# Feed-forward part of a hybrid decoder layer: arithmetic moved off GpSimd, sums of weight blocks kept in DRAM

## The chip, the cores and the metric

One core of a Trainium2 chip runs the kernel. The time is the device time of one execution in microseconds, and a kernel's time is the median over its runs. The engines are named as the profile does: PE (matrix multiplications), PEld (loads of its stationary operand, which overlap PE), DVE (vector engine), ACT (activation engine), POOL (GpSimd) and SP (which here issues most transfers). Each engine takes its instructions in the order in which they were written for it and waits on semaphores for the others.

## The reference, cut to what matters

One layer is computed in float32 for a prompt of 2048 tokens and 8 single sample tokens, model width 1024, inner width 4096. Attention and retention come first and are not touched. The part that the change concerns is this:

```python
mix = jnp.einsum('bte,ed->btd', heads, w_out)
x1 = layernorm(ALPHA * x + mix, ln1_g, ln1_b)
h = jnp.square(jax.nn.relu(jnp.einsum('btd,df->btf', x1, w_up)))
ffn = jnp.einsum('btf,fd->btd', h, w_down)
y = layernorm(ALPHA * x1 + ffn, ln2_g, ln2_b)
```

`layernorm` subtracts the mean over the 1024 features, divides by the root of the variance plus 1e-5, and applies a gain and an offset.

## The kernel before

**Precision.** A float32 product is made of three matmuls with operands that are split in a high and a low part: `wh*xh + wh*xl + wl*xh`. `split` (L344 and L349) makes the high part on ACT by a copy with rounding, and the low part on DVE as the difference. So each weight tile and each activation tile costs one ACT and one DVE instruction.

**Layout.** Features lie on the partitions, tokens along the free dimension. The 2056 tokens are taken in three passes (`NPASS`) of 688, 688 and 680 columns, each of two halves (344, 344, 340 columns, `WIDTH`), so that a PSUM bank holds one half.

**Up product.** For a pair of inner-width blocks, `up_set` uses a Strassen-like scheme: the two halves of the tokens and two blocks of the weight form a 2x2 product from seven products instead of eight. Its activation side are seven combinations `fx` of x1 blocks (named in `ORD`), made once per pass by `build` and `build_jobs`. Its weight side are seven blocks of 128x512 that `f_prep` makes for each pair: four of them are parts of `w_up`, and three more sums and differences (`t`, `a21 + a22`, `a21 + a22 - a11`) and a fourth (`a12` less the last one) are computed on POOL from the two raw tiles (L288, L289, L290, L302). The same pairs of blocks are needed in each of the three passes, and the sums are made anew in each. `product` does one of the seven products, 12 matmuls, written as `ups` at L1577 to L1579. A *cell* adds the earlier products (L1601, DVE), applies relu (L1603, ACT), and `act` squares: ACT writes the rounded high part of the square into `hid` (L1588), POOL squares in place into `rl` (L1589), and DVE writes the difference into the low part (L1590).

**Down product.** `down` multiplies `hid` with tiles of `w_down` (`dps`, L1636 to L1638) and adds to `ya` in SBUF (L1645). The order of blocks in a pass is from `f_order`: two pairs of up blocks, then for each of the eight groups one up pair, the group's down product (16 accumulations of 12 matmuls), one up pair.

**Weights.** `f_load` requests the raw tiles in the order of the list `fraws` on SP's queue (L228), three tiles ahead, into four buffers of 128x1024. `f_prep` is called by `f_ahead` four products ahead of use, and its results go to six half-size buffers (`fu`), so that ACT and DVE can split up to six products ahead of PE. A request for a tile waits at SP until the splits of the tile that lay in its buffer are done, and all that SP issues later waits with it.

**Norms and builds beside the products.** Jobs of layer norm (`ln_jobs`) and of `build` are streams. Norm 2 of pass s-1, norm 1 of pass s+1 and the build for pass s+1 run during pass s; norm 1 of pass 0 and its build run during the output projection. `tick`, called twice in a product, advances a modelled time and hands out the next job of a stream when the modelled backlog of each engine that it uses (`tf`) is no more than 4 us (`AHEAD`); `busy` adds modelled costs of other work. A final scheduler then orders the instructions of each engine. A norm has: two chains of additions over the eight feature tiles (L1156 on POOL into `lb`, L1157 on DVE), their sum (L1159), its split, the mean by a matmul with ones (`lm`, L1171), the subtraction of the mean (L1182: tiles 1 and 5 on POOL, the rest on DVE), squares on ACT (L1185), their sum (L1178, alternately POOL and DVE), the variance by a matmul (`lvv`, L1199), and the scaling (L1208 on POOL for tiles 2 and 5, L1210 on DVE for the rest). In a build, two of four differences are on POOL, two on DVE (L1540).

**At a pass's end** the group 7 of passes 0 and 1 loads the 14 `fx` operands of the next pass from DRAM. POOL issues these transfers (L1709), and POOL also issues the loads of `ya` (L1675). Each waits until PE has used the old operand.

## Time and profile before

| | |
|---|---|
| median of 3 runs | 2728.62 us (2723.07 to 2729.89) |
| the profiled execution | 2731.33 us |
| its span, first to last instruction | 2729.5 us |
| mean granted TensorE clock | 0.976 |
| PE busy | 2615.8 us, 96% |
| DVE, ACT, POOL busy | 1862.1, 1173.3, 986.6 us |
| first up product of pass 0, last down product of pass 2 | 1245.3 us, 2718.3 us |

The busy shares are means over the whole span. The time before about 1150 us belongs to attention and retention and is the same in both kernels; of the rest, some stages hold only up and down products, and others hold norms and builds besides. The windows by stage in the prediction are cut along these.

### The profile page before, as it was taken

The page shows a single profiled execution, that of the slowest core. Times are in us where ns is not written, and L with a number is a line of the kernel's source. Part 1 is how long each engine was busy: PE and PEld are TensorE (multiplying, and loading weights), DVE is VectorE, ACT ScalarE, POOL GpSimd, SP SyncE. Part 2 cuts the span into 40 slices and gives each one's busy share as a digit, 9 for nine tenths or more (in the row PEclk, how much of TensorE's full clock was granted, in tenths as well). Part 3 has the DMA queues.
Part 4 walks back from the last instruction along what each step waited for, and adds up shares of the span by engine and source line. Part 5 has one row for each costly group of instructions (what it writes and reads, how often), then busy time and mean ns, then how long its engine had stood idle before and what let it go on. Part 6 is the DMA issues. An engine that isn't in the chain of part 4 may idle for free. (4 is left out here: it accounts for less than half of the span.)

```text
span 2729.5 us, 44870 instructions
## 1 busy us (share of the span) xinstructions
PE 2615.8 (96%) x16852; PEld 2409.8 (88%) x16852; DVE 1862.1 (68%) x3411; ACT 1173.3 (43%) x2420; POOL 986.6 (36%) x849
## 2 busy tenths in 40 slices
PE   8999999999999999987989999999999999999998
PEld 7998788767787887876989999999999999999997
DVE  4667876555777667488886555679886558865557
ACT  3455344343353555354553333345543324443325
POOL 2123533312332213145543333456533335433333
PEclk8999999999999999988999999999999999999999
DMA  7445765655664445675363221833562294322211
GB/s 243 125 128 171 215 191 153 212 185 166 182 199 151 136 136 180 188 248 194 104 225 122 84 72 62 321 108 104 168 224 79 70 266 146 129 75 81 78 62 57
DMA packets 211596, 412.23 MB, mean 151 GB/s; under 512 B 31745, under 2 KB 114434, under 8 KB 210835
## 3 DMA queue, kind: packets, MB, share of 16 engines
q1 hardware_dynamic: 193252, 363.94, 41.4%
q0 software_dynamic: 14880, 40.62, 4.7%
q10 hardware_dynamic: 3248, 4.82, 0.5%
q8 instruction: 133, 2.18, 0.3%
q14 instruction: 83, 0.68, 0.1%
HBM read 323.95 MB, written 85.35 MB: 150 GB/s over the span
## 5 line engine op out<-in xcount | busy, mean ns | idle before, releaser
L1637 PE MATMUL dps<-hid,fh 128*128 128x344 f32 (+2 forms) x1544 | 494.8, 321 | 6.9 <-DVE hid L1590 6.9
L1636 PE MATMUL dps<-hid,fh 128*128 128x344 f32 (+2 forms) x1544 | 491.2, 321 | 6.9 <-ACT fh L344 5.4
L1638 PE MATMUL dps<-hid,fl 128*128 128x344 f32 (+2 forms) x1544 | 485.3, 322 | 9.9 <-DVE fl L349 8.7
L1577 PE MATMUL ups<-fx,fu 128*128 128x344 f32 (+1 forms) x1344 | 436.9, 326 | 23.4 <-ACT fu L344 8.3
L1578 PE MATMUL ups<-fx,fu 128*128 128x344 f32 (+1 forms) x1344 | 436.1, 325 | 2.9 <-DVE fx L349 2.9
L1579 PE MATMUL ups<-fx,fu 128*128 128x344 f32 (+1 forms) x1344 | 428.3, 324 | 2.5 <-DVE fu L349 2.5
L336 PE MATMUL gps<-xh,wh 128*128 128x512 f32 (+2 forms) x1120 | 402.5, 362 | 8.0 <-ACT xh L344 6.9
L338 PE MATMUL gps<-xh,wl 128*128 128x512 f32 (+2 forms) x1120 | 399.6, 358 | 4.2 <-DVE wl L349 4.2
L337 PE MATMUL gps<-xl,wh 128*128 128x512 f32 (+2 forms) x1120 | 400.4, 358 | 1.1 <-DVE xl L349 0.8
L344 ACT ACTIVATE fu<-fr 128x512 fp32r<-128x512 f32 x288 | 176.3, 627 | 309.4 <-PE dps L1637 127.8
L1638 PEld LDWEIGHTS dps<-hid,fl 128*128 128x128 f32 x1544 | 292.7, 191 | 11.3 <-DVE fl L349 9.8
L1637 PEld LDWEIGHTS dps<-hid,fh 128*128 128x128 f32 x1544 | 294.6, 191 | 7.8 <-DVE hid L1590 7.8
L1636 PEld LDWEIGHTS dps<-hid,fh 128*128 128x128 f32 x1544 | 293.3, 190 | 8.7 <-ACT fh L344 6.5
L1645 DVE TENSOR_TENSOR ya<-dps,ya 128x344 f32<-128x344 f32 (+2 forms) x344 | 168.5, 501 | 174.3 <-PE dps L1638 173.0
L1577 PEld LDWEIGHTS ups<-fx,fu 128*128 128x128 f32 x1344 | 257.9, 192 | 28.8 <-ACT fu L344 9.5
L1589 POOL TENSOR_TENSOR rl<-rl 128x344 f32<-128x344 f32 (+1 forms) x192 | 184.9, 965 | 231.9 <-ACT hid L1588 231.8
L349 DVE TENSOR_TENSOR fu<-fr,fu 128x512 fp32r<-128x512 f32 x288 | 230.0, 811 | 52.1 <-ACT fu L344 50.6
L1578 PEld LDWEIGHTS ups<-fx,fu 128*128 128x128 f32 x1344 | 257.7, 192 | 4.3 <-DVE fx L349 4.2
L1579 PEld LDWEIGHTS ups<-fx,fu 128*128 128x128 f32 x1344 | 256.5, 192 | 3.8 <-DVE fu L349 3.8
L336 PEld LDWEIGHTS gps<-xh,wh 128*128 128x128 f32 x1120 | 215.1, 193 | 46.9 <-issue 8.7
L337 PEld LDWEIGHTS gps<-xl,wh 128*128 128x128 f32 x1120 | 215.5, 193 | 35.9 <-issue 7.5
L338 PEld LDWEIGHTS gps<-xh,wl 128*128 128x128 f32 x1120 | 215.8, 193 | 35.2 <-DVE wl L349 4.6
(263 smaller groups left out, 5146.5 us busy)
## 6 DMA issues: line engine op xcount, KB each, us to landing
wr<-in_w_in SPq DMA_DIRECT2D x111, 512.0 KB
fr<-in_w_up SPq DMA_DIRECT2D x96, 512.0 KB
fr<-in_w_down SPq DMA_DIRECT2D x96, 512.0 KB
xr<-in_x SPq DMA_DIRECT2D x64, 256.0 KB
wr<-in_w_out SPq DMA_DIRECT2D x32, 512.0 KB
t<-modd SPq DMA_DIRECT2D x16, 512.0 KB
ab<-ad SPq DMA_DIRECT2D x32, 256.0 KB
xr<-hd SPq DMA_DIRECT2D x32, 256.0 KB
```

Of the source, the lines that this page charges most:

```text
L336: mm(ps, wh, xh[:, c0:c0 + n], start=(k == 0), stop=False)
L337: mm(ps, wh, xl[:, c0:c0 + n], start=False, stop=False)
L338: mm(ps, wl, xh[:, c0:c0 + n], start=False, stop=(k == last))
L344: nc.scalar.activation(h, raw, AF.Copy)
L349: (nc.vector if eng_l == "v" else nc.gpsimd).tensor_tensor(out=l, in0=raw, in1=f32(h), op=OP.subtract)
L1577: mm(ps, wh, xh[:, k, :n], start=start and k == 0, stop=False, skip_group_check=not start)
L1578: mm(ps, wh, xl[:, k, :n], start=False, stop=False, skip_group_check=not start)
L1579: mm(ps, wl, xh[:, k, :n], start=False, stop=k == 3, skip_group_check=not start)
L1589: nc.gpsimd.tensor_tensor(out=r, in0=r, in1=r, op=OP.mult)
L1636: mm(ps, wh, xh, start=(k == 0), stop=False)
L1637: mm(ps, wh, xl, start=False, stop=False)
L1638: mm(ps, wl, xh, start=False, stop=(k == 3))
```

## The change

- `act`: ACT squares `rl` in place, then ACT copies it with rounding to the high part; POOL's instruction is gone.
- `ln_jobs` and `build_jobs`: all additions, subtractions and scalings are on DVE. POOL keeps only two scalings of the very last piece of the last norm, and some sums of squares in the last group's `down`.
- `f_prep`: in pass 0 the four sums of a pair of blocks are made on DVE, and each is stored by SP to a DRAM tensor `wsd` (16 of them, 4 blocks of 128x512 each). In passes 1 and 2 nothing is summed: the raw list has four tiles for a pair (the first `w_up` tile, two tiles of stored sums, the second half of the second `w_up` tile), and further requests are placed at pieces 3 and 4 of the seven.
- The modelled costs in `busy` and in the job lists follow the engines.

```diff
 def f_open(self):
+        self.wsd = [self.dram(f"wsd{p}", [P, 4, 512]) for p in range(16)]
...
-                    self.fraws += [self.i["w_up"][4 * g + f], self.i["w_up"][4 * g + f + 1]]
-                    self.funits += [("u", b, j) for j in range(7)]
+                    t, w = 4 * g + f, self.wsd[2 * g + f // 2]
+                    if s == 0:
+                        self.fraws += [up[t], up[t + 1]]
+                    else:
+                        self.fraws += [up[t], w[:, 0:2].rearrange("p a n -> p (a n)"),
+                                       w[:, 2:4].rearrange("p a n -> p (a n)"), up[t + 1][:, 512:1024]]
+                    self.funits += [("s" if s == 0 else "u", b, j, w) for j in range(7)]
...
 def f_prep(self, q):
-            pl(out=z["t"], in0=z["a11"], in1=z["a21"], op=OP.subtract)
-            pl(out=z["a21"], in0=z["a21"], in1=z["a22"], op=OP.add)
-            pl(out=z["a11"], in0=z["a21"], in1=z["a11"], op=OP.subtract)
-            src = z["a11"]
-            self.busy(P=3.9)
...
-            pl(out=z["a12"], in0=z["a12"], in1=z["a11"], op=OP.subtract)
...
+        if kind == "u":
+            t, c = ((0, 0), (1, 0), (0, 1), (1, 1), (2, 0), (3, 0), (2, 1))[j]
+            if j in (3, 4):
+                self.f_load(b + j + 1)
+            src = self.fraw[b + t][:, 512 * c:512 * c + 512]
...
+                v(out=z["t"], in0=z["a11"], in1=z["a21"], op=OP.subtract)
+                v(out=z["a21"], in0=z["a21"], in1=z["a22"], op=OP.add)
+                v(out=z["a11"], in0=z["a21"], in1=z["a11"], op=OP.subtract)
+                self.busy(D=2.1)
+            elif j == 6:
+                v(out=z["a12"], in0=z["a12"], in1=z["a11"], op=OP.subtract)
+                self.busy(D=0.7)
+            for k, o in {1: (("a11", 0),), 3: (("t", 1),), 4: (("a21", 2),), 6: (("a12", 3),)}.get(j, ()):
+                nc.sync.dma_start(ws[:, o, :], z[k])
...
 def ln_jobs(...):
-        app_p = APP_L if last else APP_P
+        app_p = APP_L if last else ()
...
-                    p(out=c["b"], in0=c["b"] if k else z[4], in1=z[5 + k], op=OP.add)
+                    v(out=c["b"], in0=c["b"] if k else z[4], in1=z[5 + k], op=OP.add)
...
-                    (v if k % 2 else p)(out=c[k - 1], in0=c[k - 1], in1=c[k - 3], op=OP.add)
+                    v(out=c[k - 1], in0=c[k - 1], in1=c[k - 3], op=OP.add)
...
-                    (p if k in CEN_P else v)(out=z[k], in0=z[k], in1=c["m"], op=OP.subtract)
+                    v(out=z[k], in0=z[k], in1=c["m"], op=OP.subtract)
...
 def build_jobs(...):
-        return [diff("P", t3, d, b), part("B11", a, 1), diff("P", b, b, a), part("B22", d, 1), part("T3", t3, 0),
+        return [diff("D", t3, d, b), part("B11", a, 1), diff("D", b, b, a), part("B22", d, 1), part("T3", t3, 0),
...
 def act(self, hid, c, n, r):
-        nc.scalar.activation(h, r, AF.Square)
-        nc.gpsimd.tensor_tensor(out=r, in0=r, in1=r, op=OP.mult)
+        nc.scalar.activation(r, r, AF.Square)
+        nc.scalar.copy(h, r)
         nc.vector.tensor_tensor(out=l, in0=r, in1=f32(h), op=OP.subtract)
-        self.busy(A=0.49, P=0.76, D=0.51)
+        self.busy(A=0.98, D=0.51)
```

Seven lines come in ahead of `split`, `ln_jobs` and `act`, so a line L349 of the old kernel is L356 in the new one, L1156 is L1163, L1590 is L1597, and L1709 is L1716.

POOL at the end of pass 1, before: the loads of `fx` (from DRAM tensors `xd2T` and `xd2B`) and the squares of the last cells (L1589) in one queue.

```order
L1709 DMA fx_23006<-xd2T_12468 128x4x340
L1709 DMA fx_23009<-xd2T_12471 128x4x340
L1589 TENSOR_TENSOR rl_22915<-rl_22915 128x344
L1709 DMA fx_23008<-xd2T_12470 128x4x340
L1589 TENSOR_TENSOR rl_22950<-rl_22950 128x344
L1709 DMA fx_23011<-xd2T_12473 128x4x340
L1709 DMA fx_23010<-xd2T_12472 128x4x340
L1709 DMA fx_23013<-xd2B_12475 128x4x340
L1709 DMA fx_23012<-xd2B_12474 128x4x340
L1589 TENSOR_TENSOR rl_22976<-rl_22976 128x344
L1589 TENSOR_TENSOR rl_22994<-rl_22994 128x344
```

The same place of POOL's queue in the changed kernel.

```order
L1716 DMA fx_23070<-xd2T_12468 128x4x340
L1716 DMA fx_23073<-xd2T_12471 128x4x340
L1716 DMA fx_23072<-xd2T_12470 128x4x340
L1716 DMA fx_23075<-xd2T_12473 128x4x340
L1716 DMA fx_23074<-xd2T_12472 128x4x340
L1716 DMA fx_23077<-xd2B_12475 128x4x340
L1716 DMA fx_23076<-xd2B_12474 128x4x340
```

The squares have left the queue, and the loads stand one behind the other.

POOL in the second norm of pass 2 (norm 2 of pass 1, second half), before: the chain of three additions into `lb_23923` (L1156), with block sums (L288 to L290, L302) around it.

```order
L290 TENSOR_TENSOR fr_23826<-fr_23895,fr_23826 128x512
L1156 TENSOR_TENSOR lb_23923<-zc_23864 128x344
L1156 TENSOR_TENSOR lb_23923<-lb_23923,zc_23864 128x344
L288 TENSOR_TENSOR ft_24274<-fr_23970,fr_24072 128x512
L302 TENSOR_TENSOR fr_23826<-fr_23826 128x512
L1156 TENSOR_TENSOR lb_23923<-lb_23923,zc_23864 128x344
L289 TENSOR_TENSOR fr_24072<-fr_24072 128x512
```

DVE at the same place in the changed kernel, where that chain is `lb_24060` (L1163), the other one is `lsq_24059` (L1164), and L1166 adds the two. L1650 is the down product's addition to `ya`.

```order
L1164 TENSOR_TENSOR lsq_24059<-zc_23987 128x344
L1650 SCALAR_TENSOR_TENSOR ya_23358<-ya_23358,dps_24038 128x340
L1164 TENSOR_TENSOR lsq_24059<-lsq_24059,zc_23987 128x344 x2
L1650 SCALAR_TENSOR_TENSOR ya_23358<-ya_23358,dps_24052 128x340
L1163 TENSOR_TENSOR lb_24060<-zc_23987 128x344
L1163 TENSOR_TENSOR lb_24060<-lb_24060,zc_23987 128x344 x2
L1650 SCALAR_TENSOR_TENSOR ya_23358<-ya_23358,dps_24072 128x340
L356 TENSOR_TENSOR fu_24192<-fr_23946,fu_24192 128x512
L1166 TENSOR_TENSOR lsq_24059<-lsq_24059,lb_24060 128x344
```

The second chain has come from POOL to DVE, where it follows the first one, with two other operations before their sum.

DVE at the opening of pass 0, before (first build, first weight blocks).

```order
L349 TENSOR_TENSOR fu_13549<-fr_13541,fu_13549 128x512
L349 TENSOR_TENSOR fx_12485<-zc_13232,fx_12484 128x344
L1540 TENSOR_TENSOR zc_13232<-zc_13232 128x344
L349 TENSOR_TENSOR fx_12479<-zc_13232,fx_12478 128x344
L349 TENSOR_TENSOR fx_12483<-lb_13379,fx_12482 128x344
L1340 SCALAR_TENSOR_TENSOR z_13469<-xr_13362,gps_13407 128x512
L1540 TENSOR_TENSOR zc_13232<-zc_13232 128x344
L349 TENSOR_TENSOR fu_13559<-fr_13541,fu_13559 128x512
```

And in the changed kernel, from the same first low part of a weight block on.

```order
L356 TENSOR_TENSOR fu_13565<-fr_13557,fu_13565 128x512
L301 TENSOR_TENSOR ft_13568<-fr_13557,fr_13559 128x512
L302 TENSOR_TENSOR fr_13559<-fr_13559 128x512
L1547 TENSOR_TENSOR lb_13345<-zc_13304 128x344
L356 TENSOR_TENSOR fx_12489<-zc_13304,fx_12488 128x344
L303 TENSOR_TENSOR fr_13557<-fr_13559,fr_13557 128x512
L356 TENSOR_TENSOR fx_12489<-zc_13304,fx_12488 128x344
L1547 TENSOR_TENSOR zc_13304<-zc_13304 128x344
L356 TENSOR_TENSOR fx_12483<-lb_13345,fx_12482 128x344
L356 TENSOR_TENSOR fu_13573<-fr_13557,fu_13573 128x512
```

Three block sums (L301 to L303) and the builds' differences of POOL (L1547) stand between the low parts that the first products need.

More of the change, by code (lines that the diff above doesn't have):

```diff
@@ L47 @@
 ORD = ("B11", "T2", "B21", "T3", "T1", "T4", "B22")
-CEN_P = (1, 5)
-APP_P = (2, 5)
 SP = 100
@@ L208, in f_open @@
                     self.fraws.append(self.i["w_down"][g, d])
-                    self.funits.append(("c" if s == NPASS - 1 and g == 7 else "d", b, d))
+                    self.funits.append(("c" if s == NPASS - 1 and g == 7 else "d", b, d, None))
         self.flr, self.fraw, self.fq, self.fp, self.frdy, self.fpar, self.fset = 0, {}, 0, 0, {}, 0, {}
@@ L227, in f_load @@
             t = pool.tile([P, 1024], F32, tag="wr", name=self.nm("fr"), bufs=2)
-            self.nc.sync.dma_start(t, self.fraws[q])
+            src = self.fraws[q]
+            t = t[:, :src.shape[-1]]
+            self.nc.sync.dma_start(t, src)
             self.fraw[q] = t
@@ L232, in f_slots @@
     def f_slots(self, q):
-        return 1 if self.funits[q][0] == "u" else 2
+        return 1 if self.funits[q][0] in "su" else 2
     def f_next(self):
@@ L256, in f_prep @@
         nc = self.nc
-        kind, b, j = self.funits[q]
-        pl = nc.gpsimd.tensor_tensor
-        if kind != "u":
+        kind, b, j, ws = self.funits[q]
+        v = nc.vector.tensor_tensor
+        if kind not in "su":
             self.f_load(b + 3)
@@ L1159, in f @@
                     v(out=c["a"], in0=c["a"], in1=c["b"], op=OP.add)
-            return f, [("P", G, 0)] * (k < 3) + [("D", D, 0)], 1
+            return f, [("D", D * (1 + (k < 3)), 0)], 1
         def parts(x):
@@ L1207, in f @@
                     if k in app_p:
-                        p(out=z[k], in0=z[k], in1=c["r"], op=OP.mult)
+                        nc.gpsimd.tensor_tensor(out=z[k], in0=z[k], in1=c["r"], op=OP.mult)
                     else:
```

36 lines of the change are left out of this document (14 added, 22 removed).

## The prediction

> **What bounds the kernel now.** I read the page's busy shares first, then the windows by stage (columns: length, then busy us and count of PE, PEld, DVE, ACT, POOL, the granted TensorE clock, DMA share, GB/s), then who PE waited for, then the DVE groups of the stages with gaps.
>
> ```profile
> PE 2615.8 (96%) x16852; PEld 2409.8 (88%) x16852; DVE 1862.1 (68%) x3411; ACT 1173.3 (43%) x2420; POOL 986.6 (36%) x849
> ...
> 1150.00:1245.00 95.00, 85.23 (x477) 74.26 (x476) 71.89 (x105) 42.51 (x76) 36.52 (x31) 0.93 0.78 263
> 1245.00:1310.00 65.00, 47.44 (x240) 42.29 (x238) 60.81 (x77) 31.68 (x66) 39.80 (x34) 0.86 0.41 143
> 1310.00:1460.00 150.00, 138.12 (x817) 135.28 (x818) 121.74 (x190) 72.58 (x143) 70.43 (x59) 0.95 0.53 180
> 1460.00:1710.00 250.00, 250.00 (x1587) 250.00 (x1587) 143.27 (x227) 87.08 (x153) 82.27 (x69) 1.00 0.22 72
> 1710.00:2040.00 330.00, 310.93 (x1899) 307.05 (x1898) 263.59 (x397) 155.32 (x305) 167.63 (x148) 0.97 0.54 186
> 2040.00:2195.00 155.00, 155.00 (x986) 155.00 (x985) 90.35 (x143) 54.12 (x94) 50.95 (x42) 1.00 0.23 75
> 2195.00:2350.00 155.00, 143.57 (x878) 141.53 (x878) 115.08 (x166) 67.20 (x128) 84.75 (x77) 0.96 0.65 198
> 2350.00:2655.00 305.00, 305.00 (x1961) 305.00 (x1960) 185.91 (x297) 108.57 (x191) 104.84 (x87) 1.00 0.26 85
> 2655.00:2730.00 75.00, 60.55 (x426) 59.09 (x424) 55.88 (x116) 38.81 (x94) 26.62 (x26) 0.93 0.18 58
> ```
>
> TensorE sets the end, and its instructions are the same before and after, some norm matmuls at other places. Where the feed-forward part runs alone (1460-1710, 2040-2195, 2350-2655) PE is busy all the time at clock 1.00: there an edit on another engine is worth nothing, unless it spoils this. Something is to be had only where layer norms and builds run beside it. Idle (length less PE busy) and clock loss (1 less the clock, times the length) are: out projection 9.8 + 6.7, opening of pass 0 17.6 + 9.1, its norms 11.9 + 7.5, pass 1 19.1 + 9.9, pass 2 11.4 + 6.2, end 14.5 + 5.3. That is 84 + 45 us, the most that any edit here could return. In these stages DVE is busy 74% to 94% of the time, so a wait that ends on DVE, or on ACT for a DVE result, is a queue on DVE.
>
> Why that queue is long:
>
> ```profile
> L349 DVE TENSOR_TENSOR fu<-fr,fu 128x512 fp32r<-128x512 f32 x65 | 52.8, 823 | 12.4 <-ACT fu L344 12.2
> L1590 DVE TENSOR_TENSOR hid<-rl,hid 128x344 fp32r<-128x344 f32 x42 | 35.0, 838 | 6.0 <-POOL rl L1589 6.0
> L1645 DVE TENSOR_TENSOR ya<-dps,ya 128x344 f32<-128x344 f32 x64 | 31.4, 506 | 8.9 <-PE dps L1638 8.8
> L349 DVE TENSOR_TENSOR fl<-fr,fh 128x1024 fp32r<-128x1024 f32 x20 | 26.9, 1346 | 4.1 <-PE ups L1579 3.2 <-ACT fh L344 0.9
> L1210 DVE SCALAR_TENSOR_TENSOR zc<-zc,lnp,lb 128x344 f32<-128x344 f32 (+1 forms) x24 | 23.8, 1058 | 0.0
> L1182 DVE TENSOR_TENSOR zc<-zc,lm 128x344 f32<-128x344 f32 (+1 forms) x24 | 15.2, 696 | 0.0
> L1178 DVE TENSOR_TENSOR lsq<-lsq,lsq 128x344 f32<-128x344 f32 (+1 forms) x12 | 10.1, 843 | 0.5 <-ACT lsq L1185 0.4
> ...
> L349 DVE TENSOR_TENSOR fu<-fr,fu x288: 675/692/2648, 1240.2 to 2672.6; 128x512 fp32r<-128x512 f32 x144
> L349 DVE TENSOR_TENSOR fl<-fr,fh x92: 1209/1226/2353, 1309.0 to 2630.8; 128x1024 fp32r<-128x1024 f32 x92
> L1590 DVE TENSOR_TENSOR hid<-rl,hid x192: 496/512/2276, 1269.9 to 2687.0; 128x344 fp32r<-128x344 f32 x128, 128x340 fp32r<-128x340 f32 x64
> L1645 DVE TENSOR_TENSOR ya<-dps,ya x344: 319/509/519, 1379.9 to 2718.6; 128x344 f32<-128x344 f32 x112, 128x340 f32<-128x340 f32 x52, 128x170 f32<-128x170 f32 x8
> L1210 DVE SCALAR_TENSOR_TENSOR zc<-zc,lnp,lb x60: 559/568/1625, 1204.1 to 2351.9; 128x344 f32<-128x344 f32 x48, 128x340 f32<-128x340 f32 x12
> ```
>
> The first seven rows are DVE groups of pass 1's stage (the number before the second bar is the mean ns), the last five the min/median/max of a line. The same 344-wide operation takes 496 ns at best, 838 on the mean in this stage and 2276 at worst where both inputs lie in SBUF, but never over 519 where one comes from PSUM. The delay therefore is in SBUF beside POOL's arithmetic. Per stage of pass 1 the excess over the medians is 65 x 0.131 = 8.5, 42 x 0.326 = 13.7, 20 x 0.12 = 2.4, 24 x 0.49 = 11.8, and with 0.512 as the free 344-wide duration 24 x 0.184 = 4.4 and 12 x 0.33 = 4.0: 44.8 us in 330.
>
> **The change part by part.** *POOL to DVE.* DVE gets 64 sums of 128x512 (pass 0 only, 64 x 0.692 = 44 us) and 138 operations of layer norm and build (138 x 0.512 = 71 us): 10 for each of ten norms, 14 in the parts of the last two, 8 for each of three builds. Pass 1 holds four norms and a build, 48 x 0.512 = 24.6 against the 44.8 that go: DVE falls from 263.6 to about 243 of 330. Pass 2's stage: POOL is busy 84.75 against 167.6, so about 22.7 go and 10.2 come (two norms). Pass 0 from 1245 to 1460: POOL 110, so about 29.5 go, while 8 pairs of blocks bring 8 x 4 x 0.692 = 22.1, two norms 10.2 and the builds some 7: 39. DVE is then about 9 us busier, 192 of 215.
>
> *Squares to ACT.* POOL's `rl` product goes; ACT makes the square in place and a copy more.
>
> ```profile
> L1589 POOL TENSOR_TENSOR rl<-rl x192: 745/934/1742, 1265.3 to 2685.2; 128x344 f32<-128x344 f32 x128, 128x340 f32<-128x340 f32 x64
> ...
> L1603 ACT ACTIVATE rl<-rl 128x344 f32<-128x344 f32 x93 | 45.2, 488 | 68.8 <-DVE rl L1601 68.2
> ```
>
> 192 copies by 0.488 are 94 us on ACT, hidden: pass 1's stage goes from 155 to about 176 of 330, pass 0's norms from 73 to 82 of 150. Without that cover the splits `fu` and `fh` behind them on ACT would be late by 0.49 each time. A cell's chain gets shorter by 0.934 - 0.488 = 0.45 us. What this frees is POOL's queue:
>
> ```profile
> 2212.08 0.74 POOL L1709 DMA_DIRECT2D fx<-xd2T  x1 [2.43 <-DMA fx<-xd2T]
> 2215.09 1.48 POOL L1709 DMA_DIRECT2D fx<-xd2B  x2 [2.26 <-issue]
> 2216.59 1.48 POOL L1589 TENSOR_TENSOR rl<-rl 128x344 f32<-128x344 f32 x2
> 2217.39 3.78 DVE L1590 TENSOR_TENSOR hid<-rl,hid 128x344 fp32r<-128x344 f32 x2 [5.93 <-POOL rl L1589]
> ...
> PE dps L1637 <- DVE hid L1590: 6.9, 2, 4.7
> ...
> 2210.00:2220.00 10.00, 5.29 (x33) 5.00 (x33) 4.07 (x4) 0.93 (x2) 5.56 (x7) 0.85 1.41 380
> 2220.00:2230.00 10.00, 10.00 (x53) 10.00 (x54) 6.83 (x11) 1.69 (x2) 0.99 (x2) 0.81 1.40 363
> ```
>
> At the end of a pass the last squares stand behind loads of the next operands, and PE waits 4.7 us (2.2 a pass earlier). These 6.9 us go whatever DVE does, with the clock lost in the last two rows, 1.5 + 1.9: **-10.3**.
>
> *The norm's sum.* The mean's matmul stands in PE's order and waits for a chain that goes over POOL:
>
> ```profile
> 2315.28 0.93 POOL L1156 TENSOR_TENSOR lb<-zc 128x344 f32<-128x344 f32 x1 [8.22 <-DMA zc<-yd]
> 2316.29 1.26 POOL L1156 TENSOR_TENSOR lb<-lb,zc 128x344 f32<-128x344 f32 x1
> 2317.51 1.75 POOL L288 TENSOR_TENSOR ft<-fr,fr 128x512 f32<-128x512 f32 x1
> ...
> 2320.43 0.91 POOL L1156 TENSOR_TENSOR lb<-lb,zc 128x344 f32<-128x344 f32 x1
> 2321.38 1.56 DVE L1159 TENSOR_TENSOR lsq<-lsq,lb 128x344 f32<-128x344 f32 x1 [2.02 <-POOL lb L1156]
> ...
> PE lm L1171 <- ACT lsq L344: 11.1, 5, 4.3
> ...
> PE lm L1171 <- ACT lsq L344: 2.6, 2, 2.0
> ```
>
> Three additions take from 2315.3 to 2321.3, with block sums between them (of the last two rows one is the whole run's, one pass 1's stage; the 4.3 is pass 2's). On DVE they come behind the other chain's three, with two other operations before the sum: 6 x 0.512 + 2 x 0.5 = 4.1 us instead of 6.1. I take half of the 11.1 us, 5.5, and half as much in clock (the table's 45 to 84): **-8**, bounds 0 and -16.6.
>
> *DVE's backlog in passes 1 and 2.* Of 30.5 us idle, 6.9 (squares) and 2.6 + 4.3 (lm) are spoken for; 16.7 is left. With 20 us less on DVE I take half and its clock: **-12**, bounds 0 and -25. *Pass 0.* Idle 29.5, clock 16.6, and DVE 9 us busier but without operations of up to 2.3 us: bounds -25 and +25, taken **-5** since a late part on the path had one hop less. *The rest* (end, out projection): -1, bounds -9 and +6.
>
> PE's longest wait in the stage 1310-1460 was:
>
> ```profile
> PE ups L1577 <- DVE u L1619: 3.3, 1, 3.3
> ```
>
> The Trainium skill's page TensorE: Matmul & The Clock Gate (What's actually happening) lets the clock fall only after an idle window of some 3.4 us. The stage 1310-1460 lost 7.5 us of clock with this as its longest wait, so the trace does not bear that out as a strict bound; by it the backlog's term would be some 2 us smaller and the result 2699.
>
> *Sums kept in DRAM.* Pass 0 stores 64 x 256 KB; a pair of blocks in passes 1 and 2 loads 1792 KB instead of 1024, 32 times: 16.8 + 25.2 = 42 MB more. SP issues them all.
>
> ```profile
> SPq L228 <- DVE fu L349: 704.5, 89, 23.9
> ```
>
> SP's queue already waits 704 us for raw buffers; behind its new stores stand the next loads. A product is 12 matmuls of 250/1587 = 0.158 us, 1.9 us; seven products with 1792 KB need 139 GB/s, below the 380 of the row 2210-2220. Raw tiles are now asked for four pieces ahead (7.6 us) besides the six that splits run ahead of PE. Only beside the loads at a pass's opening can that be short: **+2**, bounds 0 and +8.
>
> Sum: -10.3 - 8 - 12 - 5 - 1 + 2 = -34. The profiled execution took 2731.33 us (span 2729.5); 2731.3 - 34 = **2697**. The median of the runs shown, 2728.62, is 2.7 lower.
>
> **The rivals.** (a) *DVE becomes the bound in pass 0: slower.* For: 94% busy in the opening already; its idle there is 4.2 us and the 12 sums of three pairs of blocks alone bring 8.3; in 1310-1460 idle is 28.3 and about 28 come. If the excess does not go, the opening is 7 us longer and the next stage has no slack; I price that at half of 28 and half again in clock, 7 + 14 + 10 = 31. With passes 1 and 2 returning the sure 10.3, 2731 + 31 - 10 = 2752. It decides from about 145 of 150 us busy there. Against: the 496-to-2276 spread. The Trainium skill's Perfetto Trace Analysis (Optimizing Scalar/DVE Operations) advises moving work off a saturated DVE, which speaks for this rival; it adds that between DVE and GpSimd that might not help, as they share a port, which the spread bears out. (b) *Order, not load, makes the stalls*: each is a place in PE's order, new ones come where old ones go, and only the sure part stays, less the stores: 2731 - 10 + 5 = 2726. (c) *The relief is worth more*: a stall ends once a queue is shorter than the run-ahead; then the whole of the bounds for norm and backlog comes and half of pass 0's: 2731 - 10 - 17 - 25 - 13 = 2666. (d) *Loads become late* at each opening of pass 1 and 2, +8 and as much again in two places: 2731 - 34 + 18 = 2715. That POOL's arithmetic stays is excluded: 8 instructions of it are left in this part.
>
> **How the numbers follow.** Forecast 0.50, (c) 0.18, (d) 0.05, (b) 0.13, (a) 0.14. Within 0.3% (8 us, what repeated runs can tell) of 2728.6 lies (b); faster is 0.50 + 0.18 + 0.05 = 0.73, slower 0.14. The range reaches from a little below (c) to (b): 2660 to 2728; the forecast's own is 2682 to 2712.
>
> **What would show it.** The 344-wide SBUF operations at means near 0.51; no wait of PE for `hid` at a pass's end; lm waits under 4 us in sum; DVE near 243 us in pass 1's norms; PE at 100% with clock 1.00 in the quiet stages. Wrong, if DVE is over 95% busy through 1310-1460 and PE idles there more than 12 us, or if `fu` waits for `fr` loads.

## The result, and the profile after

The changed kernel took 2651.86 us (median of 4 runs, 2645.22 to 2659.17), the kernel before 2726.7 us (4 runs): ratio 0.9727, 95% interval 0.9697 to 0.9756. The gain is 75 us where 34 were forecast. The direction was right; the time lies 8 us below the range and closest to rival (c).

The page of the changed kernel, busy time of each engine (span 2649.5 us):

```profile
PE 2583.2 (97%) x16852; PEld 2387.1 (90%) x16852; DVE 1776.2 (67%) x3613; ACT 1245.5 (47%) x2612; POOL 363.3 (14%) x327
```

DVE does 202 instructions more than before and is busy 86 us less. The same stages as in the prediction, in the windows of the changed kernel (length, then busy us and count of PE, PEld, DVE, ACT, POOL, granted clock, DMA share, GB/s):

```profile
1150.00:1234.00 84.00, 79.73 (x463) 69.69 (x463) 64.04 (x117) 38.98 (x69) 9.41 (x5) 0.98 0.85 281
1234.00:1297.00 63.00, 44.74 (x231) 40.34 (x230) 48.95 (x99) 34.74 (x74) 1.89 (x2) 0.78 0.60 202
1297.00:1450.00 153.00, 153.00 (x973) 153.00 (x972) 127.48 (x249) 86.18 (x172) 0.00 (x0) 1.00 0.60 205
1450.00:1700.00 250.00, 249.74 (x1583) 249.17 (x1582) 156.71 (x270) 107.09 (x198) 7.45 (x14) 1.00 0.42 146
1700.00:2015.00 315.00, 310.30 (x1953) 309.89 (x1952) 233.75 (x456) 175.48 (x354) 1.80 (x2) 0.99 0.60 203
2015.00:2165.00 150.00, 150.00 (x953) 150.00 (x953) 79.38 (x135) 60.31 (x110) 10.36 (x14) 1.00 0.46 145
2165.00:2310.00 145.00, 145.00 (x931) 145.00 (x930) 107.92 (x205) 77.13 (x157) 1.79 (x2) 1.00 0.65 217
2310.00:2585.00 275.00, 275.00 (x1767) 275.00 (x1766) 155.56 (x273) 112.91 (x211) 0.00 (x0) 1.00 0.31 102
2585.00:2650.00 65.00, 55.11 (x406) 54.48 (x405) 45.04 (x112) 38.70 (x97) 5.12 (x8) 0.96 0.24 76
```

The third row is the one to learn from. In the norms of pass 0 DVE is busy 127.48 of 153 us, 83%; before it was 121.74 of 150, 81%. PE lost 11.9 us there before and loses nothing now, with as full a DVE. Loss of a stage is length less PE busy, plus one less the clock times the length, as in the prediction:

| stage | loss before | after |
|---|---|---|
| out projection | 16.5 | 6.0 |
| opening of pass 0 | 26.7 | 32.2 |
| norms of pass 0 | 19.4 | 0 |
| norms of pass 1 | 29.0 | 7.9 |
| norms of pass 2 | 17.6 | 0 |
| end | 19.8 | 12.5 |

Most of the gain is in one stretch, from the first to the last down product. This is its row before, and then after:

```profile
1306.00:2718.00 1412.00, 1362.89 (x8542) 1352.74 (x8541) 974.83 (x1520) 580.54 (x1095) 587.99 (x506) 0.98 0.38 126
```

```profile
1297.00:2639.00 1342.00, 1337.04 (x8550) 1335.94 (x8548) 901.36 (x1682) 654.06 (x1286) 25.50 (x38) 1.00 0.48 162
```

It is 70 us shorter: PE idles 44 us less (49.1 to 5.0), and its matmuls take 26 us less (1362.89 to 1337.04), since the clock falls less often. The span fell by 80.0 us. Of the other 10, 11 came ahead of the first up product (1245.3 to 1234.4 us), and the opening, from there to the first down product, got 2 longer (60.3 to 62.7 us).

DVE of the changed kernel, four groups of pass 1's norms (1700 to 2015 us; mean ns before the last bar), and min/median/max of one line over the run:

```profile
L356 DVE TENSOR_TENSOR fu<-fr,fu 128x512 fp32r<-128x512 f32 x79 | 52.7, 687 | 7.1 <-ACT fu L351 6.8
L356 DVE TENSOR_TENSOR fl<-fr,fh 128x1024 fp32r<-128x1024 f32 x21 | 25.6, 1221 | 5.6 <-ACT fh L351 5.5
L1597 DVE TENSOR_TENSOR hid<-rl,hid 128x344 fp32r<-128x344 f32 x44 | 22.4, 511 | 1.9 <-ACT hid L1596 1.7
L1217 DVE SCALAR_TENSOR_TENSOR zc<-zc,lnp,lb 128x344 f32<-128x344 f32 x16 | 8.0, 572 | 0.7 <-ACT lb L1209 0.7
...
L1597 DVE TENSOR_TENSOR hid<-rl,hid x192: 502/509/524, 1268.5 to 2608.0; 128x344 fp32r<-128x344 f32 x128, 128x340 fp32r<-128x340 f32 x64
```

823 ns became 687, 1346 became 1221, 838 became 511, and 2276 at worst became 524. DVE operations with both inputs in SBUF are no longer held up. What PE still waits for between 1230 and 2650 us in the changed kernel (sum, count, longest):

```profile
PE ups L1584 <- ACT fx L351: 14.1, 3, 10.5
PE ups L1584 <- ACT p L1616: 6.8, 2, 4.7
PE ups L1584 <- ACT fu L351: 1.3, 2, 1.0
PE lvv L1206 <- DVE lsq L1658: 1.1, 1, 1.1
```

The waits for `hid`, `fl`, `fh`, `u` and, in this stretch, `lm` are gone. Two are new: 10.5 us for `fx` in the opening and 4.7 us at 1970 us.

### The profile page after: what moved, and what is told of

The parts are those of the page before. It is cut to its first block, busy times and chain, and to the rows that moved or that the text cites. A ratio compares the mean times of both kernels' runs of the same rounds, so it can differ in the third digit from the quotient of the medians.

```text
span 2649.5 us, 44699 instructions
## 1 busy us (share of the span) xinstructions
PE 2583.2 (97%) x16852; PEld 2387.1 (90%) x16852; DVE 1776.2 (67%) x3613; ACT 1245.5 (47%) x2612; POOL 363.3 (14%) x327
## 2 busy tenths in 40 slices
DMA packets 230028, 454.18 MB, mean 171 GB/s; under 512 B 33793, under 2 KB 116482, under 8 KB 229267
## 4 chain that ended last, share of the span: by engine, by line
PE 78%; DMA 9%; DVE 7%; issue 2%; POOL 1%; ACT 1%; SPq 1%; DVEq 0%; POOLq 0%; ACTq 0%
PE dps L1644 8%; PE dps L1645 8%; PE dps L1643 8%; PE ups L1584 7%; PE ups L1585 7%; PE ups L1586 7%; PE gps L343 5%; PE gps L345 5%; PE gps L344 5%; PE o L685 2%; PE ptps L654 2%; PE vps L439 2%; PE vps L440 2%; PE vps L441 2%; DMA zc<-x1d 1%
## 5 line engine op out<-in xcount | busy, mean ns | idle before, releaser
L351 ACT ACTIVATE fu<-fr 128x512 fp32r<-128x512 f32 x320 | 193.4, 627 | 339.4 <-PE dps L1644 226.1
L1644 PEld LDWEIGHTS dps<-hid,fh 128*128 128x128 f32 x1544 | 290.3, 188 | 0.0
L1643 PEld LDWEIGHTS dps<-hid,fh 128*128 128x128 f32 x1544 | 289.7, 188 | 0.1
L1584 PEld LDWEIGHTS ups<-fx,fu 128*128 128x128 f32 x1344 | 254.6, 190 | 25.3 <-ACT fx L351 15.2
L1585 PEld LDWEIGHTS ups<-fx,fu 128*128 128x128 f32 x1344 | 254.8, 190 | 2.4 <-DVE fx L356 2.4
L1586 PEld LDWEIGHTS ups<-fx,fu 128*128 128x128 f32 x1344 | 253.8, 190 | 0.8 <-DVE fu L356 0.8
L356 DVE TENSOR_TENSOR fu<-fr,fu 128x512 fp32r<-128x512 f32 x320 | 214.5, 689 | 45.4 <-ACT fu L351 43.8
L356 DVE TENSOR_TENSOR wl<-wr,wh 128x1024 fp32r<-128x1024 f32 (+1 forms) x147 | 189.8, 1297 | 57.7 <-ACT wh L351 55.3
```

Of the source, the lines that this page charges most:

```text
L351: nc.scalar.activation(h, raw, AF.Copy)
L356: (nc.vector if eng_l == "v" else nc.gpsimd).tensor_tensor(out=l, in0=raw, in1=f32(h), op=OP.subtract)
L1584: mm(ps, wh, xh[:, k, :n], start=start and k == 0, stop=False, skip_group_check=not start)
L1585: mm(ps, wh, xl[:, k, :n], start=False, stop=False, skip_group_check=not start)
L1586: mm(ps, wl, xh[:, k, :n], start=False, stop=k == 3, skip_group_check=not start)
L1643: mm(ps, wh, xh, start=(k == 0), stop=False)
```

## The experiments

**The question.** The theory after the result: what cost PE its time was DVE's *hold-up* beside POOL's reading of SBUF, not DVE's load. One rival is DVE's load, the prediction's own measure; another that PE waited for POOL's results and for what stood behind them in POOL's queue. Hold-up below means: over all additions, subtractions and multiplications of DVE between the first and the last down product, the sum of duration less the free duration of the shape, where it is over 15 ns (688 ns at 512 wide, 1220 at 1024, 507 and 502 at 344 and 340, 562 and 560 in the scalar form). It is worked out from the single instructions of each trace. All gains below are against the runs of the kernel before in the same comparison, whose median was 2719.85 to 2726.7 us.

| kernel | ratio, 95% interval | gain, us | first to last down product, us | PE idle there | DVE busy | POOL busy | hold-up |
|---|---|---|---|---|---|---|---|
| before | 1 | 0 | 1412 | 49.1 | 975 | 588 | 155 |
| squares alone | 0.992 (0.9895 to 0.9945) | 24 | 1387 | 34.7 | 936 | 394 | 119 |
| norms alone | 0.9899 (0.9868 to 0.993) | 25 | 1382 | 31.0 | 971 | 479 | 109 |
| sums alone | 0.9816 (0.9789 to 0.9843) | 52 | 1362 | 19.5 | 938 | 320 | 86 |
| sums back on POOL | 0.978 (0.9757 to 0.9803) | 57 | 1351 | 13.0 | 927 | 280 | 66 |
| norms back on POOL | 0.9758 (0.9727 to 0.9789) | 69 | 1351 | 11.7 | 906 | 143 | 52 |
| squares back on POOL | 0.9753 (0.9733 to 0.9774) | 66 | 1349 | 10.2 | 928 | 202 | 32 |
| changed, idle POOL reads | 0.9734 (0.9716 to 0.9752) | 70 | 1342 | 4.9 | 936 | 206 | 39 |
| changed, idle POOL writes | 0.9732 (0.9708 to 0.9757) | 71 | 1342 | 4.8 | 901 | 167 | 1 |
| changed, three times the idle POOL work | 0.9908 (0.9884 to 0.9931) | 24 | 1383 | 34.4 | 1051 | 571 | 160 |
| changed | 0.9727 (0.9697 to 0.9756) | 75 | 1342 | 5.0 | 901 | 26 | 1 |
| changed, sums on DVE in every pass | 0.9711 (0.9687 to 0.9735) | 80 | 1335 | 0.5 | 974 | 26 | 1 |
| changed, `ya` later | 0.9699 (0.9682 to 0.9715) | 80 | 1339 | 4.3 | 900 | 26 | 1 |
| `ya` later, sums on DVE in every pass | 0.9667 (0.9645 to 0.969) | 90 | 1333 | 0 | 973 | 26 | 1 |

In the table, "alone" is one part of the change made in the kernel before, and "back" is one part taken out of the changed kernel. An "idle" POOL operation is one added to the changed kernel whose result nobody reads. In the recorded expectations the port theory is the hold-up under another name.

**Each part alone.** The squares moved, nothing else:

```diff
 def act(...):        # the kernel before
-        nc.scalar.activation(h, r, AF.Square)
-        nc.gpsimd.tensor_tensor(out=r, in0=r, in1=r, op=OP.mult)
+        nc.scalar.activation(r, r, AF.Square)
+        nc.scalar.copy(h, r)
```

> The kernel before with one part of the change: the squares and their rounded copies on ACT, no POOL instruction in a cell. The change as a whole brought 75 us. Port theory (POOL's SBUF arithmetic holds up DVE, and PE's gaps are that delay; gain by the POOL time that goes): squares are about 181 of 584 us of POOL arithmetic in this part, so about 23 us, with hid near 510 ns only where no other POOL work runs. Queue theory (the gaps came from what stood behind in POOL's own queue): only the two waits at the ends of passes, about 10 us. Load theory (what counts is the sum of DVE's work): no DVE operation moves, so under 10 us. Threshold theory (gaps vanish only when all POOL arithmetic is gone): under 15 us here, and the three parts alone add up to much less than 75.

The sums of weight blocks alone (`f_open`, `f_load` and `f_prep` of the change in the kernel before). Of the seven blocks of a pair, three are parts of `w_up` and four are sums:

```diff
-            pl(out=z["t"], in0=z["a11"], in1=z["a21"], op=OP.subtract)
...
+                v(out=z["t"], in0=z["a11"], in1=z["a21"], op=OP.subtract)
...
+                nc.sync.dma_start(ws[:, o, :], z[k])
```

> The kernel before with one part of the change: block sums on DVE in pass 0, kept in DRAM for passes 1 and 2. Port theory: 278 of 584 us of POOL arithmetic go, so about 36 us, most of it in passes 1 and 2. Load theory: DVE gets 44 us more in pass 0 and nothing less later apart from excess, so 0 to 15 us of gain, pass 0 worse. Queue theory: norms' additions no longer stand behind block sums on POOL, so the waits for the mean (11 us) go, about 15 us. Threshold theory: under 20 us.

Norms and builds alone (`ln_jobs` and `build_jobs` of the change in the kernel before):

```diff
-                    p(out=c["b"], in0=c["b"] if k else z[4], in1=z[5 + k], op=OP.add)
+                    v(out=c["b"], in0=c["b"] if k else z[4], in1=z[5 + k], op=OP.add)
...
-        return [diff("P", t3, d, b), part("B11", a, 1), diff("P", b, b, a), part("B22", d, 1), part("T3", t3, 0),
+        return [diff("D", t3, d, b), part("B11", a, 1), diff("D", b, b, a), part("B22", d, 1), part("T3", t3, 0),
```

> The kernel before with one part of the change: norms and builds all on DVE, block sums and squares still on POOL. Port theory: about 125 of 584 us of POOL arithmetic go, so 16 us. Load theory: DVE gets 71 us more, so slower by 5 to 30 us. Queue theory: waits for the mean go, about 15 us faster. Threshold theory: 0 to 10 us.

The gains are 24, 52 and 25 us, 101 in sum, where all three together bring 75: once two are done the third has little left to save. The port theory had expected 23, 36 and 16 us: right for the squares, too low for the other two. The rows from the first to the last down product, squares alone, then sums alone, then norms alone:

```profile
1302.00:2689.00 1387.00, 1352.32 (x8542) 1342.29 (x8543) 936.39 (x1515) 654.84 (x1280) 393.74 (x321) 0.99 0.39 128
```

```profile
1301.00:2663.00 1362.00, 1342.51 (x8548) 1335.85 (x8546) 938.00 (x1573) 583.50 (x1102) 320.12 (x328) 1.00 0.48 159
```

```profile
1313.00:2695.00 1382.00, 1350.97 (x8544) 1340.92 (x8544) 970.74 (x1622) 580.84 (x1098) 478.92 (x403) 0.99 0.39 129
```

The first two have the same DVE busy time, 936 and 938, and differ by 25 us in length. DVE's load does not order these three kernels; the hold-up does (119, 86, 109).

**DVE loaded, POOL quiet.** In the changed kernel the sums are made on DVE in all three passes, with no copies in DRAM:

```diff
-                    t, w = 4 * g + f, self.wsd[2 * g + f // 2]
-                    if s == 0:
-                        self.fraws += [up[t], up[t + 1]]
-                    else:
-                        ...
-                    self.funits += [("s" if s == 0 else "u", b, j, w) for j in range(7)]
+                    t, w = 4 * g + f, None
+                    self.fraws += [up[t], up[t + 1]]
+                    self.funits += [("s", b, j, w) for j in range(7)]
...
-                nc.sync.dma_start(ws[:, o, :], z[k])
```

> The changed kernel without the DRAM copies: DVE makes the block sums in every pass, so 128 more sums of 0.69 us, 88 us more DVE work in passes 1 and 2, and 42 MB less traffic. Port theory: DVE at its undisturbed speed has room (about 234 of 315 us in the norms of pass 1, plus some 28), so passes 1 and 2 stay nearly free of gaps: 2650 to 2665. Load theory: DVE is back where it was before, so the gaps of passes 1 and 2 come back: 2690 to 2715.

And the same sums on POOL in all three passes, the rest as changed (`f_open`, `f_load` and `f_prep` of the kernel before):

```diff
-                v(out=z["t"], in0=z["a11"], in1=z["a21"], op=OP.subtract)
...
-                nc.sync.dma_start(ws[:, o, :], z[k])
...
+            pl(out=z["t"], in0=z["a11"], in1=z["a21"], op=OP.subtract)
```

> The changed kernel with the block sums back on POOL in all three passes and nothing kept in DRAM; squares on ACT and norms on DVE stay. Alone the sums brought 52 us. Port theory with POOL's longest operations (1.3 to 1.7 us each) back: 2670 to 2685. Threshold theory (one part of POOL work brings all gaps back): 2700 or more.

These two differ only in the engine that makes the sums (DVE first, POOL second):

```profile
1298.00:2633.00 1335.00, 1334.54 (x8549) 1333.30 (x8547) 973.86 (x1811) 658.18 (x1286) 25.57 (x38) 1.00 0.40 133
```

```profile
1298.00:2649.00 1351.00, 1337.97 (x8546) 1334.19 (x8544) 927.29 (x1622) 654.82 (x1284) 280.46 (x218) 1.00 0.39 132
```

With the sums on DVE it is busy 974 us, as in the kernel before, and PE has no gap. With them on POOL, DVE is busy 47 us less and PE idles 13 us. That refutes DVE's load as the measure. Both kernels came out a little faster than the port theory had expected (2646.35 us against 2650 to 2665, 2662.44 against 2670 to 2685). The pair also shows that the copies in DRAM were not needed: without them the kernel is no slower (0.9711 against 0.9727, overlapping intervals).

**POOL busy, nobody waiting for it.** One idle multiplication for each cell, reading `rl` from SBUF into a scratch tile:

```diff
         nc.vector.tensor_tensor(out=l, in0=r, in1=f32(h), op=OP.subtract)
+        nc.gpsimd.tensor_tensor(out=self.scr[:, :n], in0=r, in1=r, op=OP.mult)
```

> The changed kernel with one instruction of POOL more in each cell: it multiplies the squared tile by itself into a scratch tile that nobody reads (192 times, as many and as long as the squares before). No engine waits for its result; only the buffer of the cell is held longer, and there are five. Port theory: DVE's SBUF operations are held up again, hid maxima far over 510 ns, and part of the gaps comes back: 2660 to 2675. Queue and hop theories: nothing waits for it, so 2652 within 5.

Beside it, two idle fills of `rl`, which only write:

```diff
+        nc.gpsimd.memset(r, 0.0)
+        nc.gpsimd.memset(r, 0.0)
```

> The changed kernel with two POOL memsets of the cell's tile after its last use (384 in all, about 0.75 us for the two), so POOL is busy about as long as with the squares, but only writes SBUF. Port theory, if only reading of SBUF by POOL stands against DVE's second SBUF input: no change, 2652 within 6, hid near 510 ns. If any POOL use of SBUF does: 2660 to 2675 as with the reading one.

The row and the lines of the kernel with idle reads, then of that with idle writes (min/median/max of one):

```profile
1298.00:2640.00 1342.00, 1337.10 (x8547) 1335.99 (x8546) 935.55 (x1681) 655.07 (x1285) 205.78 (x223) 1.00 0.48 162
...
L1597 DVE TENSOR_TENSOR hid<-rl,hid x192: 496/506/1078, 1268.5 to 2610.4; 128x344 fp32r<-128x344 f32 x128, 128x340 fp32r<-128x340 f32 x64
L1598 POOL TENSOR_TENSOR scr<-rl x192: 753/835/3873, 1266.6 to 2611.6; 128x344 f32<-128x344 f32 x128, 128x340 f32<-128x340 f32 x64
```

```profile
1298.00:2640.00 1342.00, 1337.24 (x8551) 1336.31 (x8549) 901.32 (x1684) 654.23 (x1287) 166.65 (x408) 1.00 0.48 162
...
L1597 DVE TENSOR_TENSOR hid<-rl,hid x192: 501/507/519, 1269.7 to 2609.2; 128x344 fp32r<-128x344 f32 x128, 128x340 fp32r<-128x340 f32 x64
L1598 POOL MEMSET rl<- x192: 377/386/413, 1270.3 to 2609.7; 128x344 f32 x128, 128x340 f32 x64
```

Reads hold DVE up (1078 ns at worst, DVE's busy time 936 against 901 us), writes do not (519, 901). The Trainium skill's page SBUF — State Buffer (Who interferes with whom) says just that: a DVE instruction with two SBUF inputs contends with a GpSimd instruction that reads SBUF, not with one that only writes it. This trace agrees. But the 2660 to 2675 us that the port theory expected of the reads did not come: 39 us of hold-up made PE no gap and cost no time. So here hold-up has a slack to use up first; the next experiment tests that idea, which came after this result.

**How much it takes.** Three idle POOL operations for each cell, 576 in all:

```diff
+        nc.gpsimd.tensor_tensor(out=self.scr[:, :n], in0=r, in1=r, op=OP.mult)
+        for _ in range(2):
+            nc.gpsimd.tensor_tensor(out=self.scr[:, :n], in0=self.scr[:, :n], in1=self.scr[:, :n], op=OP.subtract)
```

> The changed kernel with three idle POOL multiplications or subtractions per cell into a scratch tile that nobody reads (576, the first one behind the cell's square, the others on the scratch itself), about as much POOL arithmetic as the kernel before had (575 us from the first to the last down product) and no engine waiting for POOL's results. With one per cell DVE was held up 39 us in sum and no gap of PE came. Hold-up theory (gaps come once DVE is held up by some 60 to 150 us in this part, whoever does it): hold-ups of 100 us or more and 2670 to 2725. Dependence theory (the gaps of the kernel before came from DVE and ACT waiting for POOL's results): hold-ups as large, but 2650 within 8.

Row, line and PE's longest sums of waits of this kernel:

```profile
1297.00:2680.00 1383.00, 1348.63 (x8543) 1338.78 (x8542) 1050.99 (x1680) 653.17 (x1284) 571.43 (x594) 0.99 0.46 157
...
L1597 DVE TENSOR_TENSOR hid<-rl,hid x192: 498/960/1094, 1263.1 to 2651.3; 128x344 fp32r<-128x344 f32 x128, 128x340 fp32r<-128x340 f32 x64
...
PE ups L1584 <- DVE u L1629: 7.3, 5, 4.4
PE ups L1586 <- DVE fu L356: 7.1, 6, 2.1
PE dps L1648 <- DVE fl L356: 5.8, 3, 2.9
PE lm L1178 <- ACT lsq L351: 4.5, 3, 2.7
```

DVE does the same instructions as in the changed kernel and is busy 150 us longer (1051 against 901). The waits of the kernel before are back, for `u`, `fu`, `fl` and `lm`, though nothing waits for POOL's results here. One wait for POOL is left: four times, 4.2 us in sum, ACT waits until an idle read has let go of a buffer of `rl`. The idle writes make it wait as much (4.3 us) and cost nothing, so that is not the cause. The stretch is 41 us longer than in the changed kernel. So hold-up alone makes 41 of the 70 us at the size that it had before (155 us there, 160 here). What it costs grows more than in proportion: 39 us cost nothing, 160 cost 41.

**POOL on the path.** The squares back on POOL, the rest as changed:

```diff
-        nc.scalar.activation(r, r, AF.Square)
-        nc.scalar.copy(h, r)
+        nc.scalar.activation(h, r, AF.Square)
+        nc.gpsimd.tensor_tensor(out=r, in0=r, in1=r, op=OP.mult)
```

> The changed kernel with the squares back on POOL: the same POOL work as one idle multiplication per cell, but DVE waits for its result, and ACT has 192 copies less. Hold-up theory: as with the idle ones, 2650 within 6, apart from the end of a pass, where the squares stand behind the loads of fx again (6.9 us of idle before, so up to 2660). Dependence theory: 2665 to 2675 (alone the squares brought 24 us).

```profile
1294.00:2643.00 1349.00, 1338.76 (x8547) 1335.91 (x8545) 927.76 (x1676) 579.68 (x1098) 202.11 (x222) 1.00 0.47 161
...
PE dps L1644 <- DVE hid L1597: 3.8, 2, 2.8
```

The hold-up is 32 us, less than with the idle reads (39), and POOL is busy as long (202 and 206 us). Yet the stretch is 7 us longer, and PE waits for `hid` twice again. The two places are the ends of passes 0 and 1 (1.0 us before 1720, 2.8 us between 2140 and 2200), where the squares stand behind the `fx` loads. So waiting for POOL costs something beside the hold-up: here 7 us, of which 3.8 are this wait itself.

Norms and builds back on POOL, the rest as changed:

```diff
-                    v(out=c["b"], in0=c["b"] if k else z[4], in1=z[5 + k], op=OP.add)
+                    p(out=c["b"], in0=c["b"] if k else z[4], in1=z[5 + k], op=OP.add)
...
-        return [diff("D", t3, d, b), part("B11", a, 1), diff("D", b, b, a), part("B22", d, 1), part("T3", t3, 0),
+        return [diff("P", t3, d, b), part("B11", a, 1), diff("P", b, b, a), part("B22", d, 1), part("T3", t3, 0),
```

> The changed kernel, with the 138 operations of layer norm and build that had moved to DVE back on POOL: the last of the three parts put back alone. Theory (a gap needs a hold-up above some 35 to 40 us between the first and the last down product): about 138 POOL operations that read SBUF, most of them with two inputs there, against 192 with one input in the run with idle squares (hold-up 34 us, no gap), so a hold-up of 25 to 45 us, the stage from the first to the last down product 1342 to 1350 us, and a median 70 to 65 us below the kernel before. The norm's sum term of the prediction, by contrast (the mean's matmul waits because its additions go over POOL and stand between block sums in POOL's queue): the block sums are gone from that queue here, so if the additions' way over POOL is what counts, PE's waits for lm come back with 5 us or more in sum; if the block sums between them counted, or the hold-up, they stay under 3 us.

Row, and PE's wait for the mean's operand after 1240 us:

```profile
1289.00:2640.00 1351.00, 1339.30 (x8543) 1335.61 (x8542) 905.80 (x1570) 653.24 (x1282) 142.95 (x145) 1.00 0.47 160
...
PE lm L1180 <- ACT lsq L353: 2.1, 2, 1.4
```

The stretch is 9 us longer than in the changed kernel, with a hold-up of 52 us, above the 25 to 45 expected. The opening is shorter (1238 to 1289 us against 1234 to 1297), since POOL, busy with the build, starts `ya` later (see the new stalls); the kernel is 6 us behind in gain, inside the intervals. The `lm` wait stays at 2.1 us with the additions on POOL. Where the block sums stay in POOL's queue it is longer. PE's waits for `lm` from the first down product on, in the kernel before, with the squares alone, and with norms alone:

```profile
PE lm L1171 <- ACT lsq L344: 7.1, 4, 4.3
...
PE lm L1171 <- ACT lsq L344: 8.8, 5, 3.5
...
PE lm L1169 <- ACT lsq L342: 2.9, 3, 2.2
PE lm L1169 <- DVE lsq L347: 1.3, 3, 0.7
```

So the additions' way over POOL is not by itself what made the mean late (2.1 us, at a hold-up of 52). The hold-up alone is enough for a good part: with three times the idle POOL work, where neither additions nor block sums are on POOL, the wait is 4.5 us (hold-up 160), and with norms alone, where the additions are on DVE, 4.2 us (hold-up 109). With additions and block sums in one queue it is 7.1 and 8.8 us (hold-up 155 and 119), so the queue adds something; how much, these single executions do not tell.

Put back alone, the three parts cost 9 (squares), 17 (sums) and 6 us (norms) of median, 32 in sum; taken alone they brought 101.

**The two new stalls.** In the changed kernel's opening, POOL starts the load of `ya` 14 us earlier than before (1244.0 against 1258.1), since it no longer has the build to do. It then runs beside the load for the build (`zc`). Timeline of the changed kernel (start, us, engine):

```profile
1244.02 1.89 POOL L1682 DMA_DIRECT2D ya<-x1d  x2 [49.34 <-DVE fx L356]
...
1247.28 2.28 SPq L1469 DMA_DIRECT2D zc<-x1d  x4
1257.20 0.87 ACT L351 ACTIVATE fx<-zc 128x344 fp32r<-128x344 f32 x2 [10.87 <-DMA zc<-x1d]
```

From issue to the first use 9.9 us pass, and PE waits 10.5. The experiment lets the `ya` load of pass 0 wait for the first cell:

```diff
-        for c in range(2):
-            nc.gpsimd.dma_start(self.ya[:, :, c * n:(c + 1) * n], self.x1d[s][:, c])
+        if s:
+            for c in range(2):
+                nc.gpsimd.dma_start(self.ya[:, :, c * n:(c + 1) * n], self.x1d[s][:, c])
...
+                if s == 0 and g == 0 and i == 0:
+                    for c in range(2):
+                        y = self.ya[:, :, c * n:(c + 1) * n]
+                        nc.gpsimd.tensor_copy(y[:, 0, 0:1], f32(hid[0][0])[:, 0:1])
+                        nc.gpsimd.dma_start(y, self.x1d[s][:, c])
```

> The changed kernel with the load of ya for pass 0 held back: it is issued by POOL once a cell of the first pair of blocks is there, instead of beside the build's load of x1d. In the changed kernel that load took 10 us and PE stood 10.5 us for it, then ran 27 us at half clock. If the two transfers collide: PE's gap in the opening falls to under 4 us and the time by 10 to 25 us. If the build's load is late for another reason: no change.

Timeline, PE's wait in the opening and the opening's row of this kernel:

```profile
1243.02 1.85 SPq L1469 DMA_DIRECT2D zc<-x1d  x4
1246.72 0.87 ACT L351 ACTIVATE fx<-zc 128x344 fp32r<-128x344 f32 x2 [4.65 <-DMA zc<-x1d]
...
1257.89 1.88 POOL L1702 DMA_DIRECT2D ya<-x1d  x2
...
PE ups L1584 <- ACT fx L351: 7.7, 3, 4.3
...
1231.00:1287.00 56.00, 44.58 (x233) 40.63 (x232) 48.73 (x99) 34.47 (x74) 2.51 (x4) 0.82 0.63 220
```

The data are used 3.7 us after issue, the longest wait is 4.3 (under 4 was expected), the opening 7 us shorter. The kernel takes 2640.26 us, beside 2649.57 and 2648.62 us for the two idle ones of the same comparison, which are as fast as the changed kernel. The collision is shown. With norms and builds back on POOL it is absent too; `ya` there starts after the build's data are in use:

```profile
1246.27 0.87 ACT L353 ACTIVATE fx<-zc 128x344 fp32r<-128x344 f32 x2 [0.92 <-DMA zc<-x1d]
...
1249.54 1.90 POOL L1684 DMA_DIRECT2D ya<-x1d  x2 [13.71 <-DMA zc<-x1d]
```

The other stall is in pass 1's build. In the changed kernel ACT waits 4.17 us for a store of the build to finish, and the copy `p`, for which PE waits, is behind that:

```profile
1969.49 0.49 ACT L351 ACTIVATE lsq<-lb 128x340 fp32r<-128x340 f32 x1 [4.17 <-DMA xd2B<-lsq]
1969.89 0.43 ACT L1616 COPY p<-ups 128x344 f32<-128x344 f32 x1
```

With the sums on DVE in every pass, which spares 42 MB of transfers (454.18 against 412.21 MB), this stall is absent (0.5 us idle in the whole stretch). That the extra traffic made the store late is not shown, though: with norms and builds back on POOL the copies are still made and the stall is absent too, and in the kernel before, which makes no copies, ACT waits up to 3.6 us for such a store. Both remedies together, by the two diffs shown for them:

> Both edits that were faster than the changed kernel: the load of ya held back in pass 0 (2640 alone), and the block sums on DVE in all passes without DRAM copies (2646 alone). If they act at different places (the opening of pass 0; the stall of 4.7 us in pass 1 beside the stores of the build): 2632 to 2638. If both act by less traffic in the opening: about 2640.

```profile
1287.00:2620.00 1333.00, 1333.00 (x8545) 1333.00 (x8545) 972.76 (x1807) 655.59 (x1285) 25.52 (x38) 1.00 0.39 133
```

From the first to the last down product PE is busy without a gap at clock 1.00. The kernel takes 2632.92 us, ratio 0.9667 (0.9645 to 0.969), which beats both kernels.

## Why the prediction was right or wrong

The direction held, and so did the cause that it named: DVE operations delayed in SBUF beside POOL's arithmetic. The size did not: 34 us were forecast and 75 measured, below the whole range.

| term | forecast | measured |
|---|---|---|
| squares behind the `fx` loads | -10.3 | PE's waits for `hid` gone; put back, the stretch is 7 longer |
| norm's sum | -8 | wait 11.1 to 2.4; with half as much in clock -13 |
| DVE's backlog, passes 1 and 2 | -12 | about -26 (what is left over, see below) |
| pass 0 | -5 | norms -19.4, opening +5.5: -14 |
| the rest | -1 | end -7.3, out projection -10.5 less 2.7 for `lm`: -15 |
| sums in DRAM | +2 | the stall at 1970 us, 4.7 and its clock: about +8, if it is theirs |
| sum | -34 | -70; the span fell by 80.0 |

The measured column is an estimate from the table of losses. Passes 1 and 2 fell by 21.1 + 17.6 = 38.7; less 10.3 for the squares (as forecast; not measured apart) and 10.4 for `lm` (2.6 + 4.3 us, and half as much in clock), and with the 8 of the new stall put back, 26 are left for the backlog. Of the other 1.8 us by which `lm` fell, 1.6 are in the out projection; the 1.8 are 2.7 with clock. The 10 us between the sum and the span are not assigned; with the clock unrounded the losses fall by 72, so rounding explains 2 of them. Measured directly is the stretch from the first to the last down product: 44 us less idle and 26 us less of slower matmuls, a clock share of 0.59 of the idle time where the prediction took half.

**The step that failed** is "With 20 us less on DVE I take half and its clock", and beside it pass 0, "DVE 9 us busier". Both price the gaps by how full DVE is. The runs show the hold-up in its place: with DVE at 974 us, as full as before, and no POOL reads, PE has no gap; with 160 us of hold-up and the changed kernel's own instructions, the gaps are back. Hence the whole bound of the backlog came (26 against 25), and pass 0, taken as nearly even since DVE's load stayed, lost all 19.4 us of its norms' gaps. The prediction had the right quantity in hand, the excess of 44.8 us over the medians in pass 1's norms (59 by the definition of hold-up used here), but used it only to lower DVE's load by 20 us net, as if the operations that came in exchange cost as much as the delay that went.

A third term failed by being put near nothing without a reason: "the rest", taken as -1 with bounds -9 and +6, came to about -15. Most of it is the out projection. In the traces, its last 380 matmuls up to the first up product take 83.5 to 85.3 us in the four kernels with norms and builds on POOL, and 74.6 to 77.7 us in the ten that have them on DVE. The hold-up over these matmuls is 16.0 to 17.6 us in the four and 3.0 to 5.8 us in the ten. So this part comes with the norms' and builds' move, by the same cause in all likelihood.

**The norm's sum.** Of 11.1 us of waits 2.4 are left, where half was taken. The prediction's picture, a chain over POOL with block sums between its additions, is part of the cause at most: hold-up alone, with neither on POOL, brings 4.5 us of these waits back.

**Sums in DRAM.** The place was wrong. At the openings of passes 1 and 2 PE waits for no weight tile. The stall that came is at 1970 us, where ACT stands behind a store of the build; without the copies it is gone and the stretch 7 us shorter, but why that store was late stays open.

**The opening of pass 0** got 5.5 us worse by the table (2.4 us by the time between the first up and the first down product), but not by rival (a): DVE idles 14 us there. POOL, free of the build, started `ya` early and met the build's load. The prediction had not asked what an idle POOL would begin sooner.

**The rivals.** (a) is refuted: in the norms of pass 0 DVE is busy 83% and PE 100%. The Trainium skill's page Perfetto Trace Analysis (Optimizing Scalar/DVE Operations) says that offloading a saturated DVE, even to GpSimd, may make sense, but that between these two engines it might not help. The runs bear out the caution: here the work on POOL cost time (2726.7 against 2651.86 us). (b) is refuted by the gaps that vanished in all norm stages. (d) did not happen. (c), "the relief is worth more", describes what happened, and was given 0.18; its 2666 us lack what the out projection brought.

**What was to be seen.** The 344-wide SBUF operations at 0.51: yes, 511. No wait for `hid`: yes. `lm` under 4 us: yes, 2.4, in the out projection:

```profile
PE lm L1178 <- ACT lsq L351: 2.4, 1, 2.4
```

DVE near 243 us in pass 1's norms: 233.75 of a shorter stage. Quiet stages at 100% and clock 1.00: yes.

**What stays open.** Of the 70 us, 41 are shown as hold-up alone, and 7 come with the squares on POOL (at a hold-up of 32 us, which as idle reads cost nothing). The other 20 or so were seen only where something also waits for POOL's results; how they divide between the norms' additions, the block sums and the cells was not separated, and since the parts do not add up, these sizes are rough.
